# Attention outputs of the samples with two head pairs per matmul, and ten weight splits moved from GpSimd to VectorE

## The chip, the cores and the metric

The kernel runs on one core of a Trainium2 chip. The time is the device time of one execution in microseconds (us). A core has five engines that run side by side, each through its own queue in order: TensorE (PE in the profile; its weight loads are listed apart as PEld), VectorE (DVE), ScalarE (ACT), GpSimd (POOL) and SyncE (SP), which only starts transfers. They wait for each other through semaphores.

## The reference

One inference step of a hybrid encoder layer for one prompt of 512 frames and 8 samples of 16 frames, 640 rows of width 1024:

```python
z = rmsnorm(x) @ w_in                     # columns: u 512, gate 512, q 512, k 128, v 128
lru_out  = rg_lru(causal_conv(u)) * gelu(gate)
attn_out = sliding_window_attention(rmsnorm(q), rmsnorm(k), v, sinks)   # 8 heads of 64, 2 key-value heads
h = x + concat(rmsnorm(lru_out), rmsnorm(attn_out)) @ w_out
y = h + peer(rmsnorm(h))                  # 8 heads, top 16 of 16384 single-neuron experts
```

The attention of a sample reads its 128 cached keys and values and its own 16:

```python
s = einsum('btgrd,bkgd->bgrtk', q, k) * 64 ** -0.5       # 2 groups g, 4 heads r in each
p = sink_softmax(s, sink)
o = einsum('bgrtk,bkgd->btgrd', p, v)                     # 64 x 16 for each sample and head
```

Everything is fp32.

## The kernel before, in words

All matmuls of weights run in three passes over a split: a number is cut into a high part `wh` (type fp32r, made by ScalarE in line 95) and a low rest `wl = raw - wh` (line 100, on the engine that the caller names), and TensorE adds high by high, high by low and low by high. The weights of the projections come as slabs of 128 x 2048. `next_slab(engine)` takes the next slab that SyncE has loaded, issues the high copy on ScalarE and the subtraction on the engine named, and asks SyncE for a further slab. Raw slabs, high parts and low parts have two buffers each.

The order on each engine is the order of the program text; no planner moves anything in the part that is changed. The stages are:

1. 0 to 36 us: keys and values of all rows, projected as the input arrives.
2. 36 to 200 us: the queries of the first four heads, the four slices of `u` with the convolution on VectorE (lines 365 to 376), the gates of the recurrence, its scan, and the prompt's attention in eight pieces (`Prompt`: scores, softmax, division, transposes, outputs), laid between the projections.
3. 200 to 275 us: `merge`, the product with `w_out`, one bank of 512 columns in 12 matmuls of 512 columns (line 622). VectorE takes each bank out into `rows` (line 628) or `h_rows` (line 636). The samples' attention is laid between: class `Samples` for samples 0 to 3 (`sm[0]`) and 4 to 7 (`sm[1]`).
4. 275 to 430 us: queries of the experts and their top keys. 5. 430 us to the end: the dense pass over all experts for the prompt and the gathered rows of the samples.

TensorE writes its results to PSUM. Four banks, tag `pb`, go round among scores, transposes, outputs and merges; two double banks, tag `pa`, serve the projections. A bank comes free when its reader (ScalarE or VectorE) is through.

In `Samples.outputs` the probabilities lie transposed in `pT` (keys by head and frame, 128 columns for a sample), so one key-value group of one sample has 64 neighbouring columns: two halves `hp` of 32, each with two heads of 16 frames. For each sample, group and half, one matmul takes 128 cached values (weights 128 x 64) and a second one the sample's own 16 (weights 16 x 64); both add into the same 64 PSUM partitions, the lower ones for one half and the upper ones for the other, because `oT` wants the heads so. That is 4 x 2 x 2 x 2 = 32 matmuls of 32 columns for one call, and in the trace each fp32 matmul is two passes. ScalarE then copies the whole bank into `oT` (line 580) in one instruction.

Of the kernel before, what the change touches and what calls it, by code (L numbers as in the profile page):

```python
# [12 lines left out]
AF = mybir.ActivationFunctionType  # L13
# [6 lines left out]
S = 512  # L20
NB, TS = 8, 16
# [27 lines left out]
def hybrid_layer(ctx: ExitStack, tc: tile.TileContext, i, o):  # L49
    nc = tc.nc  # L50
    V, A, G, PE = nc.vector, nc.scalar, nc.gpsimd, nc.tensor
# [17 lines left out]
    def bank():  # L69
        return pss.tile([P, 512], F32, name="pb", tag="pb", bufs=4)  # L70
# [22 lines left out]
    def high(raw):  # L93
        wh = stream.tile([P, 2048], F32R, name="wh", tag="wh")
        A.activation(wh, raw, AF.Copy)  # L95
        return wh

    def low(raw, wh, eng):
        wl = stream.tile([P, 2048], F32R, name="wl", tag="wl")
        eng.tensor_sub(wl, raw, wh.bitcast(F32))  # L100
        return wl
# [109 lines left out]
    def fetch_slab():  # L211
        n = len(slab_raw)
        if n < len(order):
            slab_raw.append(load_slab(order[n]))

    def next_slab(eng):

        raw = slab_raw[len(slabs)]
        wh = high(raw)
        slabs.append((wh, low(raw, wh, eng)))  # L220
        fetch_slab()
# [20 lines left out]
    qT, oT = qo[:, 0:4, :], qo[:, 4:8, :]  # L242
# [25 lines left out]
    def project_heads(c, t, s):  # L268
        ps = bank()[:, :256]
        for k in range(KD):  # L270
            project_rows(kc(slabs[s]), k, t, ps)
        heads_rows(c, t, ps)
# [24 lines left out]
    V.tensor_scalar(gqs, small["gq"], HD ** -0.5, None, op0=ALU.mult)  # L297

    project_heads(0, 0, 0)
    next_slab(G)  # L300
    project_heads(0, 1, 0)
    rb1 = rs1.spread(dg1)
    for t in range(2, NT):
# [4 lines left out]
    vown = wk.tile([TS, NB, P], F32, name="vown", tag="twice")  # L308
# [52 lines left out]
    def convolve(ct, ps, amid):  # L361
        u = wk.tile([P, UL], F32, name="u", tag="u", bufs=2)
        G.memset(u[:, 0:3], 0.0)
        G.tensor_copy(segs(u)[:, :, 0:3], small["st_conv"][:, ct])
        V.tensor_mul(u[:, 3:3 + H2], ps[:, 0, :H2], rb1[:, :H2])
        V.tensor_mul(u[:, 3 + H2:S + 3], ps[:, 1, :S - H2], rb1[:, H2:S])
        V.tensor_mul(segs(u)[:, :, 3:], ps[:, 1, S - H2:H2].rearrange("p (b s) -> p b s", s=TS),
                     rb1[:, S:].rearrange("p (b s) -> p b s", s=TS))
        G.tensor_copy(cst[:, ct, 0, :], u[:, S:S + 3])
        G.tensor_copy(cst[:, ct, 1:, :], segs(u)[:, :, TS:])  # L370
        cw = small["conv_w"]
        xc = xcs[ct] = wk.tile([P, UL], F32, name="xc", tag=("xc", "sq")[ct // 2], bufs=2)
        V.tensor_scalar(xc[:, X], u[:, X], cw[:, ct, 0:1], small["conv_b"][:, ct:ct + 1],
                        op0=ALU.mult, op1=ALU.add)
        for j in range(1, 4):
            V.scalar_tensor_tensor(xc[:, X], u[:, j:j + XL], cw[:, ct, j:j + 1], xc[:, X],
                                   op0=ALU.mult, op1=ALU.add)
            if j == 1:
                amid()
# [26 lines left out]
    def lru_weight(pair):  # L406
        for ct in pair:
            r, ig, a, q = rg[ct]
            V.tensor_mul(q[:, X], a[:, X], a[:, X])
            V.scalar_tensor_tensor(q[:, X], q[:, X], 1.0, r[:, X], op0=ALU.add, op1=ALU.mult)  # L410

    def lru_root(pair):
        for ct in pair:
            A.activation(rg[ct][3][:, X], rg[ct][3][:, X], AF.Sqrt)

    def lru_scan(pair):
        for ct in pair:
            r, ig, a, q = rg[ct]
            V.tensor_mul(ig[:, X], ig[:, X], q[:, X])
            G.memset(heads_of(a), 0.0)  # L420
            G.tensor_copy(heads_of(ig), small["st_lru"][:, ct])
            if ct == 0:
                hs["all"] = wk.tile([P, CT, UL], F32, name="hall", tag="hall")
            h = hs[ct] = hs["all"][:, ct]
            V.tensor_tensor_scan(h[:, X], a[:, X], ig[:, X], 0.0, ALU.mult, ALU.add)
            G.tensor_copy(lst[:, ct, 0:1], h[:, S - 1:S])
            G.tensor_copy(lst[:, ct, 1:], segs(h)[:, :, TS - 1])

    def project(s, n, between=()):
        ps = wide()  # L430
        for k in range(KD):
            proj_T(ps, kc(slabs[s]), xh, xl, n, (k,))
            if k < len(between):
                between[k]()
        return ps
# [17 lines left out]
    rows2 = (slice(0, 64), slice(64, 128))  # L453

    class Prompt:
# [49 lines left out]
        def outputs(self):  # L505
            n, nk, k0, hh, pT = self.n, self.nk, self.k0, self.hh, self.pT
            po = bank()[:, :2 * P].rearrange("p (b q) -> p b q", b=2)
            for h4 in range(4):
                for kt in range(nk):
                    PE.matmul(po[rows2[h4 % 2], h4 // 2], v_sb[:, k0 + kt, hh * HD:(hh + 1) * HD],  # L510
                              pT[:, h4, kt, :], start=(kt == 0), stop=(kt == nk - 1))
            A.activation(oT[:, 2 * hh:2 * hh + 2, n * P:(n + 1) * P], po, AF.Copy)
# [5 lines left out]
    class Samples:  # L518
# [43 lines left out]

        def outputs(self):
            pT = self.pT
            po = bank()[:, :4 * 4 * TS]
            pov = po.rearrange("p (a b t) -> p a b t", a=4, b=4)
            for b4 in range(4):
                b = 4 * self.hb + b4
                for g in range(2):
                    gd = slice(g * HD, (g + 1) * HD)  # L570
                    for hp in range(2):
                        c = slice((2 * g + hp) * 32, (2 * g + hp + 1) * 32)
                        out = pov[rows2[hp], 2 * g:2 * g + 2, b4, :]
                        PE.matmul(out, vc[:, b, gd], pT[:, 0, b4, c].rearrange("p (a t) -> p a t", a=2),
                                  start=True, stop=False)
                        PE.matmul(out, vown[:, b, gd], pT[:TS, 1, b4, c].rearrange("p (a t) -> p a t", a=2),
                                  start=False, stop=True)

            c0 = S + self.hb * 4 * TS
            A.activation(oT[:, :, c0:c0 + 4 * TS], po.rearrange("p (a q) -> p a q", a=4), AF.Copy)  # L580


    rows_x, rv_a, rv_h = {}, *[wk.tile([P, NT], F32, name=n) for n in ("rv_a", "rv_h")]
# [42 lines left out]
    def merge_lru_out(hf, t, ps):  # L626
        x = rows_x[t][:, hf * 512:(hf + 1) * 512]
        V.scalar_tensor_tensor(x, ps, rl[:, t:t + 1], x, op0=ALU.mult, op1=ALU.add)

    def merge_lru(hf, t):  # L630
        merge_lru_out(hf, t, merge(L0 + hf, t, 0))

    def merge_attn(hf, t):
        ps = merge(A0 + hf, t, CT)
        cs = slice(hf * 512, (hf + 1) * 512)
        V.scalar_tensor_tensor(h_rows[:, t, cs], ps, ra[:, t:t + 1], rows_x[t][:, cs], op0=ALU.mult, op1=ALU.add)
# [17 lines left out]
    pr[0][0].scores()  # L654
    pr[0][0].softmax()
    convolve(0, pu0, pr[0][0].divide)
    next_slab(G)
    pu1 = project(U0, 1)

    exchange(pr[0][0], pr[0][1])  # L660
    convolve(1, pu1, pr[0][1].divide)
    pu2 = project(U1, 0)
    next_slab(G)

    exchange(pr[0][1], pr[0][2])
    convolve(2, pu2, pr[0][2].divide)
# [5 lines left out]
    for t in range(NT):  # L672
        project_heads(1, t, Q1)
        if t == 1:
            pr[0][3].turn()
            next_slab(G)
            lru_weight(A01)
        if t == 2:
            pr[0][3].outputs()
        if t == 3:  # L680
            lru_root(A01)
    heads_norm(1)
    lru_scan(A01)
    next_slab(G)
    pg = project(G0, 0)
    for u in range(2):
        heads_turn(qkv[1], qT[:, 2 + u], gqs, u)
# [4 lines left out]
    a, b, c, d = pr[1]  # L692
# [9 lines left out]
    sq0 = attn_square(0)  # L702
    lru_decay(A23)
    lru_weight(A23)
    next_slab(G)
    pg = project(G1, 0)
    attn_sum(0, sq0)

# [9 lines left out]
    vc = wk.tile([P, NB, P], F32, name="vc", tag="vc")  # L718
# [33 lines left out]
    sm[0].scores()  # L752
    rs.add(sqs[0])
    rl = rs.rows()
    next_slab(G)
    merge_lru_out(0, 0, ps0)
    ps1 = merge(L0, 1, 0)
    d.turn()
# [11 lines left out]
    sm[1].divide()  # L770
    sm[0].outputs()
    merge_lru_out(0, 3, ps3)
    next_slab(G)
    merge_lru(0, 4)
    sm[1].turn()
    ps0 = merge(L0 + 1, 0, 0)
# [13 lines left out]
    nc.sync.dma_start(o["ncv"], cst)  # L790
    nc.sync.dma_start(o["nlr"], lst)
    merge_lru(1, 4)
    next_slab(G)


    h_rows = big.tile([P, NT, D], F32, name="h_rows", tag="acc")
# [23 lines left out]

    for t in range(NT):
        merge_attn(0, t)
    next_slab(G)
    for t in range(ND):
        merge_attn(1, t)
        nc.sync.dma_start(Hd[t], h_rows[:, t])
# [48 lines left out]
    for name in ("sk1", "sk2"):  # L875
        t = ta.tile([P, NK], F32, name=name)
# [43 lines left out]
    for u in range(2, 2 * PH):  # L920
        c, n = u // 2, u % 2
# [256 lines left out]
    used, c = 0.0, 2  # L1178
# [117 lines left out]
    po = [vps.tile([P, 512], F32, name="po", tag=f"po{k}") for k in range(KD)]  # L1296
# [126 lines left out]
```

## Time and profile before

| what | number |
|---|---|
| three timed runs | 1806.92, 1795.57, 1801.92 us; median 1801.92 |
| the profiled execution | 1800.01 us, its span 1798.2 us |
| DVE busy | 1417.0 us (79%) |
| ACT busy | 689.5 us (38%) |
| POOL busy | 723.0 us (40%) |

An engine's busy share is a mean over stages with different bounds. What a part is worth is read from its own stage: where TensorE, which does most of the work, stands still or runs at its lower clock, and what it waits for there. In the timeline a row may merge several instructions of one line ("x2" behind them); the bracket at its end says how long the engine stood idle in front of it and what released it. The column PEclk of the windows is the granted TensorE clock as a share of 2.4 GHz, so 0.50 is 1.2 GHz.

### The profile page before, as it was taken

The page shows a single profiled execution, that of the slowest core. Times are in us where ns is not written, and L with a number is a line of the kernel's source. Part 1 is how long each engine was busy: PE and PEld are TensorE (multiplying, and loading weights), DVE is VectorE, ACT ScalarE, POOL GpSimd, SP SyncE. Part 2 cuts the span into 40 slices and gives each one's busy share as a digit, 9 for nine tenths or more (in the row PEclk, how much of TensorE's full clock was granted, in tenths as well). Part 3 has the DMA queues.
Part 4 walks back from the last instruction along what each step waited for, and adds up shares of the span by engine and source line. Part 5 has one row for each costly group of instructions (what it writes and reads, how often), then busy time and mean ns, then how long its engine had stood idle before and what let it go on. Part 6 is the DMA issues. An engine that isn't in the chain of part 4 may idle for free.

```text
span 1798.2 us, 24867 instructions
## 1 busy us (share of the span) xinstructions
PE 1710.4 (95%) x9698; PEld 1563.8 (87%) x9698; DVE 1417.0 (79%) x2332; ACT 689.5 (38%) x792; POOL 723.0 (40%) x493
## 2 busy tenths in 40 slices
PE   8989999999999998899999999899999899999998
PEld 7877789998988897888888888899899799999998
DVE  7875435998666988889888877688888788888887
ACT  5456323323444443454455544222322222223232
POOL 5343222321010434344334434465555455554552
PEclk9998889999999999999999999999999999999999
DMA  5212124113454897999799999999999899999995
GB/s 163 97 46 103 41 77 145 61 58 125 169 204 171 311 356 269 309 363 359 253 347 358 356 331 374 412 366 377 373 392 382 332 386 383 379 378 388 383 364 219
DMA packets 180982, 492.68 MB, mean 274 GB/s; under 512 B 16816, under 2 KB 75056, under 8 KB 170224
## 3 DMA queue, kind: packets, MB, share of 16 engines
q1 hardware_dynamic: 58416, 231.01, 35.4%
q0 software_dynamic: 55296, 201.35, 29.2%
q10 hardware_dynamic: 67152, 58.73, 9.6%
q8 instruction: 76, 1.25, 0.3%
q14 instruction: 42, 0.34, 0.1%
HBM read 426.11 MB, written 65.48 MB: 273 GB/s over the span
## 4 chain that ended last, share of the span: by engine, by line
PE 39%; DVE 31%; ACT 8%; issue 8%; DMA 7%; ACTq 2%; POOL 1%; DVEq 0%; SPq 0%; POOLq 0%
PE pa L941 18%; DVE wl L100 9%; DVE h_rows L1162 8%; PE po L1317 6%; PE pa L113 6%; DMA Gd<-stage 4%; PE pb L622 3%; DVE at L1230 3%; ACT ph L1235 3%; DVE h_rows L1157 2%; ACTq L1247 2%; ACT wh L95 2%; DMA at<-Ad 2%; PE pb L1112 2%; DVE ring L1157 2%
## 5 line engine op out<-in xcount | busy, mean ns | idle before, releaser
L941 PE MATMUL pa<-xh,wh 128*128 128x448 f32 x1024 | 382.6, 374 | 27.0 <-ACT act L1244 27.0
L100 DVE TENSOR_TENSOR wl<-raw,wh 128x2048 fp32r<-128x2048 f32 x127 | 290.4, 2288 | 138.4 <-ACT wh L95 137.3
L1317 PE MATMUL po<-ph,wh 128*128 128x448 f32 x1024 | 376.4, 368 | 7.2 <-ACT ph L1235 6.0
L1317 PE MATMUL po<-pl,wh 128*128 128x448 f32 x1024 | 377.7, 369 | 5.8 <-DVE pl L1237 5.8
L941 PE MATMUL pa<-xh,wl 128*128 128x448 f32 x1024 | 377.6, 369 | 4.3 <-DVE wl L100 4.3
L941 PE MATMUL pa<-xl,wh 128*128 128x448 f32 x1024 | 377.7, 369 | 0.0
L1317 PE MATMUL po<-ph,wl 128*128 128x448 f32 x1024 | 376.0, 367 | 0.0
L95 ACT ACTIVATE wh<-raw 128x2048 fp32r<-128x2048 f32 x146 | 280.0, 1918 | 224.5 <-PE po L1317 110.1
L1150 POOL DMA_INDIRECT h_rows<-in_u_rows,rowi x96 | 142.5, 1484 | 340.0 <-DVE h_rows L1157 246.8
L941 PEld LDWEIGHTS pa<-xh,wh 128*128 128x128 f32 x1024 | 194.7, 190 | 46.3 <-ACT act L1244 30.8
L1317 PEld LDWEIGHTS po<-pl,wh 128*128 128x128 f32 x1024 | 193.5, 189 | 26.8 <-DVE pl L1237 10.7
L1317 PEld LDWEIGHTS po<-ph,wh 128*128 128x128 f32 x1024 | 193.6, 189 | 23.7 <-ACT ph L1235 6.4
L941 PEld LDWEIGHTS pa<-xh,wl 128*128 128x128 f32 x1024 | 194.6, 190 | 21.1 <-DVE wl L100 4.7
L1150 POOL DMA_INDIRECT ring<-in_u_rows,rowi x96 | 140.0, 1459 | 172.3 <-DVE ring L1157 149.3
L941 PEld LDWEIGHTS pa<-xl,wh 128*128 128x128 f32 x1024 | 194.9, 190 | 15.6
L1317 PEld LDWEIGHTS po<-ph,wl 128*128 128x128 f32 x1024 | 193.5, 189 | 15.4
L1150 POOL DMA_INDIRECT h_rows<-in_v,rowi x96 | 147.6, 1537 | 144.1 <-DVE h_rows L1162 121.1
L1150 POOL DMA_INDIRECT ring<-in_v,rowi x96 | 148.5, 1547 | 121.6 <-DVE h_rows L1162 100.3
L1235 ACT ACTIVATE ph<-at 128x896 fp32r<-128x896 f32 x64 | 61.0, 953 | 335.9 <-DVE at L1230 335.9
L1244 ACT ACTIVATE act<-pa 128x448 f32<-128x448 f32 x128 | 69.9, 551 | 203.7 <-PE pa L941 197.7
L100 POOL TENSOR_TENSOR wl<-raw,wh 128x2048 fp32r<-128x2048 f32 x19 | 88.2, 4642 | 147.3 <-ACT wh L95 147.3
L1120 ACT ACTIVATE stage<-pb 128x512 f32<-128x512 f32 x112 | 112.0, 1118 | 69.2 <-PE pb L1112 56.8
(270 smaller groups left out, 2563.7 us busy)
## 6 DMA issues: line engine op xcount, KB each, us to landing
raw<-in_u SPq DMA_DIRECT2D x64, 1024.0 KB, 5.8
raw<-in_v SPq DMA_DIRECT2D x64, 1024.0 KB, 8.6
Ad<-act ACTq DMA_DIRECT2D x64, 448.0 KB, 7.0
Gd<-stage ACTq DMA_DIRECT2D x28, 1024.0 KB, 12.3
gt<-Gd SPq DMA_DIRECT2D x64, 448.0 KB, 9.2
at<-Ad SPq DMA_DIRECT2D x64, 448.0 KB, 10.2
raw<-in_w_query SPq DMA_DIRECT2D x8, 1024.0 KB, 4.8
raw<-in_w_out SPq DMA_DIRECT2D x4, 1024.0 KB, 4.7
```

The source lines that it names most:

```text
L95: A.activation(wh, raw, AF.Copy)
L100: eng.tensor_sub(wl, raw, wh.bitcast(F32))
L113: PE.matmul(ps[:, hf, :H2], a[:, k, cs], b[:, k, hf * H2:(hf + 1) * H2], start=(k == 0 and n == 0), stop=(k == KD - 1 and n == 2))
L622: PE.matmul(ps, a[:, k0 + k, ts_], b[:, k, :], start=(k == 0 and n == 0), stop=(k == CT - 1 and n == 2))
L941: PE.matmul(u_ps[c, n][:, :SD], a[:, k, n * P:(n + 1) * P], b[:, k, :SD], start=(k == 0 and m == 0), stop=(k == KD - 1 and m == 2))
L1120: A.activation(d["stage"][:, :, t0:t0 + 4].rearrange("p j t -> p t j"), d[n, f], AF.Copy, scale=1.0 / GSC)
L1150: G.indirect_dma_start(out=rows[n], out_offset=None, in_=table, in_offset=bass.IndirectOffsetOnAxis(ap=rowi[:, c:c + 1], axis=0))
L1157: V.scalar_tensor_tensor(row, row, 1.0, xrow[:, n // NS_], op0=ALU.mult, op1=ALU.mult, accum_out=dots[:, n:n + 1])
L1162: V.scalar_tensor_tensor(y, row, slots[:, c:c + 1], y, op0=ALU.mult, op1=ALU.add)
L1235: A.activation(ph, a2, AF.Copy)
L1244: A.activation(act[c][:, n], u_ps[c, n][:, :SD], AF.Gelu_apprx_tanh)
L1317: PE.matmul(po[k][:, :SD], a[:, j, k * P:(k + 1) * P], b[:, j, :], start=(c == 0 and j == 0 and n == 0), stop=(c == NS - 1 and j == 1 and ...
```

## The change

Ten calls `next_slab(G)` become `next_slab(V)`: the low parts of those ten slabs are now subtracted by VectorE, at the same place of the program text. Nine subtractions stay on GpSimd (slab 11 on, in stage 4).

In `Samples.outputs` one matmul now takes all 64 columns of a group, both halves `hp`, so there are 4 x 2 x 2 = 16 matmuls of 64 columns for one call. The 64 PSUM partitions are now chosen by the parity `up` of the sample. So that every head still ends in its place in `oT`, four VectorE copies, one for each pair of half and parity, move the results (64 partitions by 128 elements each), in place of the one ScalarE instruction.

```diff
     project_heads(0, 0, 0)
-    next_slab(G)
+    next_slab(V)
     project_heads(0, 1, 0)
...
         def outputs(self):
             pT = self.pT
-            po = bank()[:, :4 * 4 * TS]
-            pov = po.rearrange("p (a b t) -> p a b t", a=4, b=4)
-            for b4 in range(4):
-                b = 4 * self.hb + b4
+
+            po = bank()[:, :8 * 2 * TS]
+            pov = po.rearrange("p (h g a b t) -> p h g a b t", h=2, g=2, a=2, b=2)
+            for b2 in range(2):
                 for g in range(2):
                     gd = slice(g * HD, (g + 1) * HD)
-                    for hp in range(2):
-                        c = slice((2 * g + hp) * 32, (2 * g + hp + 1) * 32)
-                        out = pov[rows2[hp], 2 * g:2 * g + 2, b4, :]
-                        PE.matmul(out, vc[:, b, gd], pT[:, 0, b4, c].rearrange("p (a t) -> p a t", a=2),
+                    cols = slice(2 * g * 32, 2 * (g + 1) * 32)
+                    for up in range(2):
+                        b4 = 2 * b2 + up
+                        b = 4 * self.hb + b4
+                        out = pov[rows2[up], :, g, :, b2, :]
+                        PE.matmul(out, vc[:, b, gd], pT[:, 0, b4, cols].rearrange("p (h a t) -> p h a t", h=2, a=2),
                                   start=True, stop=False)
-                        PE.matmul(out, vown[:, b, gd], pT[:TS, 1, b4, c].rearrange("p (a t) -> p a t", a=2),
+                        PE.matmul(out, vown[:, b, gd],
+                                  pT[:TS, 1, b4, cols].rearrange("p (h a t) -> p h a t", h=2, a=2),
                                   start=False, stop=True)
 
-            c0 = S + self.hb * 4 * TS
-            A.activation(oT[:, :, c0:c0 + 4 * TS], po.rearrange("p (a q) -> p a q", a=4), AF.Copy)
+            own = oT[:, :, S + self.hb * 4 * TS:S + (self.hb + 1) * 4 * TS].rearrange(
+                "p a (b u t) -> p a b u t", b=2, u=2)
+            pos_ = po.rearrange("p (h a b t) -> p h a b t", h=2, a=4, b=2)
+            for hp in range(2):
+                for up in range(2):
+                    V.tensor_copy(own[rows2[hp], :, :, up, :], pos_[rows2[up], hp])
...
     convolve(0, pu0, pr[0][0].divide)
-    next_slab(G)
+    next_slab(V)
     pu1 = project(U0, 1)
...
         if t == 1:
             pr[0][3].turn()
-            next_slab(G)
+            next_slab(V)
             lru_weight(A01)
...
```

The other seven places are the same edit: behind the second convolution slice, behind the first scan, behind `lru_weight(A23)`, behind `rs.rows()`, behind the fourth merge, behind `merge_lru(1, 4)` and behind `merge_attn(0, 4)`.

VectorE's queue behind the convolution of slice 0 of `u` (`xc`), in front of the second prompt piece's softmax (`mx`); the piece of the difference:

```order
 L493 TENSOR_TENSOR p<-p,den 128x4x128
 L376 SCALAR_TENSOR_TENSOR xc<-u,conv_w,xc 128x664 x2
+L100 TENSOR_TENSOR wl<-raw,wh 128x2048
 L477 TENSOR_REDUCE mx<-pb 128x2 x2
 L479 SCALAR_TENSOR_TENSOR mx<-mx,nsink 128x4
```

The subtraction now stands between the last two convolution steps and the softmax's maxima; before, it was GpSimd's and VectorE went on at once.

VectorE's queue around the samples' outputs and the merges, before (`psm` are the samples' probabilities, `rows` the merged rows, `xl` the low part of the attention's output):

```order
L553 TENSOR_TENSOR psm<-psm,dens 128x576
L628 SCALAR_TENSOR_TENSOR rows<-pb,rr,rows 128x512 x4
L596 SCALAR_TENSOR_TENSOR xl<-qo,ga,xh 128x512 x4
L601 TENSOR_SCALAR rv_a<-pb 128x1
L628 SCALAR_TENSOR_TENSOR rows<-pb,rr,rows 128x512
L596 SCALAR_TENSOR_TENSOR xl<-qo,ga,xh 128x128 x4
```

And of the change (line 635 was 628, 603 was 596, 608 was 601; `qo` holds `oT`):

```order
L553 TENSOR_TENSOR psm<-psm,dens 128x576
L587 COPY qo<-pb 64x4x2x16 x4
L635 SCALAR_TENSOR_TENSOR rows<-pb,rr,rows 128x512
L100 TENSOR_TENSOR wl<-raw,wh 128x2048
L635 SCALAR_TENSOR_TENSOR rows<-pb,rr,rows 128x512
L587 COPY qo<-pb 64x4x2x16 x4
L635 SCALAR_TENSOR_TENSOR rows<-pb,rr,rows 128x512 x2
L603 SCALAR_TENSOR_TENSOR xl<-qo,ga,xh 128x512 x4
```

The four evictions of merged rows, which stood in a block, now stand behind the copies of the samples' outputs and behind one subtraction.

## Rows read from the trace of the kernel before

**Rows 1.** The page, part 1: busy time, share, instructions of the engines
```profile
PE 1710.4 (95%) x9698; PEld 1563.8 (87%) x9698; DVE 1417.0 (79%) x2332; ACT 689.5 (38%) x792; POOL 723.0 (40%) x493
```

**Rows 2.** Windows: us, busy PE, PEld, DVE, ACT, POOL, then PEclk, DMA share, GB/s
```profile
200.00:220.00 20.00, 20.00 (x115) 16.45 (x114) 2.58 (x6) 4.97 (x13) 0.54 (x1) 0.74 0.08 27
132.00:136.00 4.00, 2.35 (x7) 1.91 (x8) 1.18 (x4) 3.96 (x13) 0.00 (x0) 0.55 0.72 262
```

**Rows 3.** Timeline of PE, where it had stood idle: start, us, line, [idle before <-releaser]
```profile
54.39 1.28 PE L279 MATMUL pb<-ident,qraw 128*128 128x128 f32 x10 [2.13 <-DVE sp L333]
83.59 0.82 PE L393 MATMUL pb<-xc,wi 128*128 128x332 f32 x2 [1.09 <-ACT p L485]
121.07 1.28 PE L279 MATMUL pb<-ident,qraw 128*128 128x128 f32 x10 [1.16 <-DVE qraw L265]
133.65 1.47 PE L393 MATMUL pb<-xc,wi 128*128 128x332 f32 x2 [5.45 <-ACT p L485]
171.26 0.38 PE L468 MATMUL pb<-mask_k,mask_q 64*128 64x256 f32 x1 [2.21 <-DVE rv_a L601]
```

**Rows 4.** The page, part 5: the subtraction of the low parts on each engine
```profile
L100 DVE TENSOR_TENSOR wl<-raw,wh 128x2048 fp32r<-128x2048 f32 x127 | 290.4, 2288 | 138.4 <-ACT wh L95 137.3
L100 POOL TENSOR_TENSOR wl<-raw,wh 128x2048 fp32r<-128x2048 f32 x19 | 88.2, 4642 | 147.3 <-ACT wh L95 147.3
```

**Rows 5.** Timeline of DVE, 40 to 160 us: instructions beside GpSimd's subtractions, and alone
```profile
40.42 3.26 DVE L295 TENSOR_TENSOR kn<-qraw,gkb 128x256 f32<-128x256 f32 x1
...
59.80 0.28 DVE L367 TENSOR_TENSOR u<-pa,rb 128x128 f32<-128x128 f32 x1
...
62.68 6.17 DVE L376 SCALAR_TENSOR_TENSOR xc<-u,conv_w,xc 128x664 f32<-128x664 f32 x2
...
86.17 1.85 DVE L376 SCALAR_TENSOR_TENSOR xc<-u,conv_w,xc 128x664 f32<-128x664 f32 x2
...
106.04 5.13 DVE L410 SCALAR_TENSOR_TENSOR q<-q,rg 128x664 f32<-128x664 f32 x1
...
126.87 4.20 DVE L479 SCALAR_TENSOR_TENSOR mx<-mx,nsink 128x4 f32<-128x4 f32 x1
...
157.31 1.29 DVE L477 TENSOR_REDUCE mx<-pb 128x2 f32<-128x512 f32 x2 [1.34 <-PE pb L469]
158.64 2.40 DVE L479 SCALAR_TENSOR_TENSOR mx<-mx,nsink 128x4 f32<-128x4 f32 x1
```

**Rows 6.** Chain of work that ended last, 133 to 140 us: start, us, line
```profile
133.65 1.47 PE pb L393 x2
135.12 1.60 PE pa L113 x6
...
139.41 0.56 PE pb L393 x2
139.97 0.88 PE pa L113 x6
```

**Rows 7.** Timeline of PE: starts of both output calls, and prompt outputs of 128 columns
```profile
77.41 1.14 PE L510 MATMUL pb<-pT,v_sb 128*64 128x128 f32 x16
...
203.74 0.30 PE L574 MATMUL pb<-pTs,vc 128*64 128x32 f32 x2
...
203.97 0.30 PE L576 MATMUL pb<-pTs,vown 16*64 16x32 f32 x2
...
221.73 0.30 PE L574 MATMUL pb<-pTs,vc 128*64 128x32 f32 x2
```

**Rows 8.** Chain of work that ended last: the merges behind the outputs, and later ones
```profile
213.01 5.17 PE pb L622 x12
...
231.48 4.53 PE pb L622 x12
...
236.79 35.52 PE pb L622 x156
```

**Rows 9.** Timeline of ScalarE: the high copy behind the fourth merge
```profile
218.22 1.92 ACT L95 ACTIVATE wh<-raw 128x2048 fp32r<-128x2048 f32 x1 [4.79 <-PE pb L622]
```

More of the change, by code (lines that the diff above doesn't have):

```diff
@@ L675, in hybrid_layer @@
             pr[0][3].turn()
-            next_slab(G)
+            next_slab(V)
             lru_weight(A01)
@@ L683, in hybrid_layer @@
     lru_scan(A01)
-    next_slab(G)
+    next_slab(V)
     pg = project(G0, 0)
@@ L704, in hybrid_layer @@
     lru_weight(A23)
-    next_slab(G)
+    next_slab(V)
     pg = project(G1, 0)
@@ L754, in hybrid_layer @@
     rl = rs.rows()
-    next_slab(G)
+    next_slab(V)
     merge_lru_out(0, 0, ps0)
@@ L772, in hybrid_layer @@
     merge_lru_out(0, 3, ps3)
-    next_slab(G)
+    next_slab(V)
     merge_lru(0, 4)
@@ L792, in hybrid_layer @@
     merge_lru(1, 4)
-    next_slab(G)
+    next_slab(V)
     h_rows = big.tile([P, NT, D], F32, name="h_rows", tag="acc")
@@ L822, in hybrid_layer @@
         merge_attn(0, t)
-    next_slab(G)
+    next_slab(V)
     for t in range(ND):
```

## The prediction

> **What bounds the kernel now.** I read the page first, then windows of 20 us, then the waits of TensorE and VectorE in the windows that stood out. TensorE is busy 95% of the span [rows 1], so a change pays only where TensorE stands still, where it does work that goes away, or where it runs at its lower clock. All that is edited lies between 36 and 275 us; from there on the program is the same, and whatever TensorE gains by then moves everything behind it forward.
>
> Two things are to be seen there. First, TensorE stands idle at five points [rows 3], and at four of them what released it hangs on VectorE's queue. VectorE in turn loses time whenever GpSimd subtracts: an instruction of four elements per row takes 4.20 us beside such a subtraction, two steps of the convolution 6.17 us where the same two take 1.85 us alone [rows 5]. The excess, 4.0 and 4.3 us, is nearly GpSimd's whole 4.64 us [rows 4]: VectorE does not run slower, it is held until GpSimd is through. Secondly, between 200 and 240 us TensorE is never idle, yet its clock is 0.74 of full over 200 to 220 us [rows 2]; this is where the samples' outputs run.
>
> **The sum, part 1: the subtractions.** VectorE needs 2.29 us for what GpSimd does in 4.64 us [rows 4]. Where the two collided, VectorE therefore trades a hold of 4 us or more for 2.29 us of its own. Along the chain:
>
> - Slab 1. VectorE's `kn` took 3.26 us beside GpSimd. It has 256 elements per row; 128 take 0.28 us [rows 5], so some 0.5 us alone. Then 3.26 - 0.5 - 2.29 = 0.5 us are won, and the stall at 54.39 us shrinks by 0.5.
> - Slabs 2 and 3. Each pair of convolution steps loses 6.17 - 1.85 = 4.3 us of hold and gets 2.29 us of subtraction: 2.0 us each, so VectorE and the softmax behind it are over 3 us earlier near 82 us. The stall of 1.09 us at 83.59 us [rows 3], a wait for a bank that ScalarE's exponentials read, goes wholly. TensorE is 1.6 us ahead.
> - Slab 4. `q` (line 410) took 5.13 us; at 128 x 664 it takes like a convolution step 0.92 us alone [rows 5]. 5.13 - 0.92 - 2.29 = 1.9 us; some 0.6 us of it is lost because VectorE now waits in its queue for ScalarE's high copy, which GpSimd used to wait for. 1.3 us stay, VectorE is 2.9 us ahead. The square roots and the queries of the last row tile then are late next and pass on 2.5 us, so the stall of 1.16 us at 121.07 us shrinks to 0.2 and TensorE is 2.5 us ahead.
> - Slab 5. The maximum's rescaling took 4.20 us where a free one takes about 0.2 us: 4.2 - 0.2 - 2.29 = 1.7 us. The stall of 5.45 us shrinks to 3.7 us, and TensorE is 2.5 + 1.7 = **4.2 us** ahead.
> - Slab 6. The rescaling took 2.40 us. The reductions (1.29 us and a small one, 1.5 us together) that ran beside GpSimd's subtraction now run behind VectorE's: 4.64 - 2.29 - 1.5 = **0.8 us**, off the stall of 2.21 us at 171.26 us.
> - Slab 7 to 10 stand among the merges, where TensorE has no such stalls. I cost them at nothing. Cover: a merge lasts 35.52 / 13 = 2.73 us [rows 8] and four banks go round, so an eviction may come two merges late before TensorE waits.
>
> Behind the stall of 5.45 us TensorE ran at 0.55 of full clock [rows 2]. From 133.65 to 139.41 us it did two rounds of two gate and six projection matmuls, 5.76 us; a round at full clock is 0.56 + 0.88 = 1.44 us [rows 6]. The fall cost 5.76 - 2.88 = 2.9 us. Whether 3.7 us of idleness still make it fall no row tells. So nothing or 2.9 us comes back; I take half, **1.4 us**.
>
> **Part 2: the outputs.** One call lasts from 203.74 to 213.01 us, 9.27 us, the other from 221.73 to 231.48 us, 9.75 us [rows 7, 8]; together 19.0 us. At full clock a matmul of two passes with 32 columns starts 203.97 - 203.74 = 0.23 us behind the one before. Sixteen of these remain per call. If columns cost nothing, a call takes 16 x 0.23 = 3.7 us; if the time goes with the columns, 7.3 us. I take the first end with a little added: the prompt's outputs, 128 columns with weights of the same form, need only 1.14 / 16 = 0.07 us per pass [rows 7] against 0.115 here, so the time is not in the columns, and six passes of 320 columns in 0.88 us [rows 6] give 0.46 ns per column, hence 32 x 2 x 0.46 = 0.03 us per matmul. 16 x 0.26 = 4.1 us per call; 19.0 - 8.2 = **10.8 us** won, bounds 19.0 - 14.6 = 4.4 and 19.0 - 7.4 = 11.6.
>
> The Trainium skill, "TensorEngine Tiling (Array Packing)", section Instruction Overhead, says that a matmul has some 60 cycles of overhead, so that one column is as dear as sixty. By that the call would take an estimated 16 x 0.23 x 64/60 = 3.9 us and the sum would be 0.4 us more; the trace's 0.07 us for 128 columns is nearer to that than to proportional cost.
>
> The merges behind both calls ran at the low clock, 5.17 and 4.53 us where one takes 2.73: 2.4 + 1.8 = 4.2 us. The first fall came in the middle of the call; a call half as long may end before the clock falls or at that moment. Again between nothing and 4.2 us, half: **2.1 us**.
>
> **Part 3: the copies.** Four copies of 128 elements cost about 0.28 us each [rows 5], 1.1 us per call, and ScalarE is rid of one instruction. Behind them on VectorE stand the eviction of merge (0,3), then the subtraction of slab 8, which must wait for ScalarE's 1.92 us copy behind the fourth merge [rows 9], then the eviction of merge (0,4): it comes 1.92 + 2.29 = 4.2 us later than now. Waiting for that bank would be the third merge on; between lie eight transposes, a merge of 2.73 us and 4.1 us of outputs. Hidden; without the cover it would cost 4.2 us once. The readers of `oT` get it 0.7 us later and TensorE needs their result two merges on.
>
> **Sum**: 4.2 + 0.8 + 1.4 + 10.8 + 2.1 = 19.3 us, 1800.0 - 19.3 = **1780.7**, say 1781 us. The profiled execution, 1800.01 us, lies 1.9 us under the median of the runs, 1801.92 us, well inside their spread of 11 us.
>
> **The rivals.**
>
> A. *The forecast*, 1777 to 1786 us: chance 0.52.
>
> B. *The low clock stays and columns cost.* Part 1 gives 5.0 us, no clock comes back, the calls take nearer 7.3 us: 5.0 + 4.4 = 9.4, 1790.6 us. For it: short matmuls are still what runs there, and the clock fell in both calls. Against: the 128-column row. Chance 0.22.
>
> C. *VectorE's queue eats part 1*: the subtractions wait for ScalarE in front of urgent work, as slab 4's does. Only part 2 remains, 12.9 us, 1787 us. Against: the holds of 4 us are on the page as times, and they go for certain. Chance 0.15.
>
> D. *GpSimd is held instead.* The hold works both ways if the one that starts first wins: then VectorE's 2.29 us delay GpSimd's small instructions on the chain, the powers of `heads_norm` in front of the stalls at 54.39 and 121.07 us. At most 2 x 2.29 = 4.6 us go back, 1785.3 us. The Trainium skill, "SBUF — State Buffer", section Who interferes with whom, has this rule: a VectorE instruction with two inputs in SBUF and a GpSimd instruction that reads SBUF lock each other out, whichever comes second. The trace agrees on VectorE's side (4.20 us for four elements); no row shows GpSimd held for long. Against: in the new order both powers start behind the subtraction's end. Chance 0.06.
>
> E. *Slower: VectorE becomes the bound from 36 to 275 us.* If the held instructions were waiting for something else anyway, nothing comes back for the ten subtractions, 22.9 us; four of them wait for ScalarE's 1.92 us first, 7.7 us, and the copies add 8 x 0.28 = 2.2 us. 32.8 - 10.8 = 22 us more, 1822 us. It decides once VectorE's evictions lag two merges, 5.5 us, behind TensorE. Against: VectorE is busy 2.58 of 20 us where the merges begin [rows 2]. Chance 0.05.
>
> **The numbers.** The likeliest is A, **1781 us**. B and C lie under the top of the range; with 5 us of spread on either side of A's full gain (all clock back: 22.8 us, 1777 us) and of B I get **1771 to 1796 us**. Within 1% is what a measurement of this kernel cannot tell from no change: 18 us, above 1784 us. A lies mostly past that, D and C mostly not: faster by over 1% 0.52, within 1% 0.43, slower 0.05.
>
> **What would show it.** Right: no VectorE instruction of a few elements over 1 us between 40 and 160 us; the stall at 83 us gone, the one at 121 us under 0.5 us, the one at 133 us near 3.7 us; each call of the outputs about 4 us for 32 passes; merges behind them at 2.7 us. Wrong: passes of the new matmuls at twice 0.115 us, a granted clock of 0.5 behind the calls as before, TensorE waiting on VectorE's `rows` between 190 and 260 us, or VectorE idle for ScalarE's high copy in front of the softmax.

## The result, and the profile after

The changed kernel takes **1776.13 us** (median of 4 runs, 1773.37 to 1778.53), the kernel before on the same chip 1800.36 us (4 runs, 1795.57 to 1806.92): ratio **0.9862**, 95% interval 0.9826 to 0.9899. Measured a second time, in other runs of both kernels, it was 0.987 (0.9833 to 0.9906). The profiled execution took 1778.0 us with a span of 1776.2 us, 22.0 us less than before. Of the kernels below, two of the six runs of the one with three changes took 3247 and 5580 us, for which I have no cause; they count in its median and not in its ratio.

The page's first part answers [rows 1]. TensorE loses 9.7 us of busy time, and its share of the shorter span is 96% in place of 95%; GpSimd loses 35.3 us, VectorE 2.5 us, though it took over ten subtractions of 2.29 us: more time went out of its other rows than subtraction came in.

```profile
PE 1700.7 (96%) x9634; PEld 1553.2 (87%) x9634; DVE 1414.5 (80%) x2350; ACT 688.8 (39%) x790; POOL 687.7 (39%) x483
```

TensorE's timeline, where it had stood idle (start, us, line, idle before and what ended it). Of the five stalls of [rows 3] three are left, of 0.80, 3.62 and 0.80 us; those of 1.09 and 1.16 us are gone:

```profile
52.36 1.28 PE L279 MATMUL pb<-ident,qraw 128*128 128x128 f32 x10 [0.80 <-DVE sp L333]
127.31 1.47 PE L393 MATMUL pb<-xc,wi 128*128 128x332 f32 x2 [3.62 <-ACT p L485]
164.22 0.38 PE L468 MATMUL pb<-mask_k,mask_q 64*128 64x256 f32 x1 [0.80 <-DVE rv_a L608]
```

VectorE's timeline, the instructions of [rows 5] that had stood beside GpSimd's subtractions: 3.26 has become 0.41 us, 6.17 has become 1.85, 5.13 has become 0.85, 4.20 has become 0.17, 2.40 has become 0.16.

```profile
39.65 0.41 DVE L295 TENSOR_TENSOR kn<-qraw,gkb 128x256 f32<-128x256 f32 x1
...
60.64 1.85 DVE L376 SCALAR_TENSOR_TENSOR xc<-u,conv_w,xc 128x664 f32<-128x664 f32 x2
...
105.49 0.85 DVE L410 SCALAR_TENSOR_TENSOR q<-q,rg 128x664 f32<-128x664 f32 x1
...
121.59 2.27 DVE L100 TENSOR_TENSOR wl<-raw,wh 128x2048 fp32r<-128x2048 f32 x1
...
124.56 0.17 DVE L479 SCALAR_TENSOR_TENSOR mx<-mx,nsink 128x4 f32<-128x4 f32 x1
...
153.82 0.16 DVE L479 SCALAR_TENSOR_TENSOR mx<-mx,nsink 128x4 f32<-128x4 f32 x1
```

The chain of waits through the outputs (start, us, line), against [rows 7, 8]. A call now runs from 197.46 to 201.56 us, 4.10 us for 16 matmuls of two passes; the other, from 209.72 to 213.82 us, also 4.10 us. The merge behind the first call is still slow, 4.54 us, the one behind the second is not, 2.95 us. The long row of merges starts at 217.56 in place of 236.79 us: **19.2 us** earlier.

```profile
197.46 0.26 PE pb L576 x2
197.72 0.25 PE pb L578 x2
...
201.56 4.54 PE pb L629 x12
...
209.72 0.26 PE pb L576 x2
...
213.82 2.95 PE pb L629 x12
...
217.56 35.52 PE pb L629 x156
```

The windows (us, busy PE, PEld, DVE, ACT, POOL, then PEclk, DMA share, GB/s) against [rows 2]: the granted clock over 200 to 220 us rose from 0.74 to 0.91 (it is 0.72 over 201 to 207 us, where the slow merge runs, and 1.00 over the second call and its merge); behind the stall of 3.62 us it fell as it had behind 5.45 us.

```profile
200.00:220.00 20.00, 20.00 (x108) 15.79 (x108) 9.95 (x17) 7.13 (x12) 0.00 (x0) 0.91 0.26 83
...
128.00:132.00 4.00, 4.00 (x13) 3.31 (x12) 0.80 (x2) 2.87 (x5) 0.00 (x0) 0.50 0.02 4
```

### The profile page after: what moved, and what is told of

Same layout as the page of the kernel before. It is cut to its first block, busy times and chain, and to the rows that moved or that the text cites. A ratio compares the mean times of both kernels' runs of the same rounds, so it can differ in the third digit from the quotient of the medians.

```text
span 1776.2 us, 24745 instructions
## 1 busy us (share of the span) xinstructions
PE 1700.7 (96%) x9634; PEld 1553.2 (87%) x9634; DVE 1414.5 (80%) x2350; ACT 688.8 (39%) x790; POOL 687.7 (39%) x483
## 4 chain that ended last, share of the span: by engine, by line
PE 54%; DVE 20%; DMA 7%; ACT 7%; issue 5%; ACTq 2%; POOL 1%; DVEq 0%; SPq 0%; POOLq 0%
PE po L1324 24%; PE pa L948 16%; PE pa L113 6%; DMA Gd<-stage 5%; DVE wl L100 5%; PE pb L629 3%; DVE h_rows L1169 3%; DVE h_rows L1164 2%; DVE ring L1164 2%; ACTq L1254 2%; ACT stage L1127 2%; ACT wh L95 2%; DMA gt<-Gd 2%; PE pb L1119 1%; DVE at L1237 1%
## 5 line engine op out<-in xcount | busy, mean ns | idle before, releaser
L100 DVE TENSOR_TENSOR wl<-raw,wh 128x2048 fp32r<-128x2048 f32 x137 | 313.2, 2287 | 141.6 <-ACT wh L95 135.8
L1157 POOL DMA_INDIRECT ring<-in_u_rows,rowi x96 | 145.3, 1514 | 160.9 <-DVE ring L1164 137.8
L1244 DVE TENSOR_TENSOR pl<-at,ph 128x896 fp32r<-128x896 f32 x64 | 69.9, 1092 | 72.9 <-ACT ph L1242 72.9
```

What stands on the lines that cost most here:

```text
L1157: G.indirect_dma_start(out=rows[n], out_offset=None, in_=table, in_offset=bass.IndirectOffsetOnAxis(ap=rowi[:, c:c + 1], axis=0))
L1244: V.tensor_sub(pl, a2, ph.bitcast(F32))
```

## The experiments

Whole times of one kernel differ by up to 20 us from run to run (before, on one chip: 1789.11 to 1809.14 us), so each kernel is also read at a mark in its trace, behind which nothing is edited. It is the matmul of the dense pass (line 941 before, 948 after) that waits some 4.3 us for a low part of VectorE; the expectations call it the first block of the dense pass. That line's first matmul runs 25.5 us earlier (at 407.43 us before, 388.19 us after), and distances read there are the same within 0.03 us, but for the kernel with all subtractions on VectorE. A second mark, VectorE's line 265, lies ahead of every edit and starts between 35.99 and 37.97 us; "net" is the distance between the two, less that of before (432.94 - 37.60 = 395.34 us).

| Kernel | Median, us (before on the same chip) | Ratio, 95% interval | Dense pass, us | Net, us | From there to the end |
|---|---|---|---|---|---|
| before | 1800.36 | | 432.94 | 0 | 1365.3 |
| the change | 1776.13 (1800.36) | 0.986, 0.983 to 0.990 | 413.68 | -18.5 | 1362.5 |
| the change again | 1775.23 (1799.45) | 0.987, 0.983 to 0.991 | 413.31 | -19.6 | 1361.4 |
| outputs only | 1784.89 (1795.12) | 0.994, 0.992 to 0.996 | 418.23 | -13.1 | 1365.8 |
| subtractions only | 1787.74 (1795.12) | 0.995, 0.994 to 0.997 | 426.43 | -6.9 | 1366.8 |
| added subtractions | 1789.35 (1799.45) | 0.995, 0.992 to 0.998 | 423.45 | -8.1 | 1359.0 |
| added memsets | 1775.14 (1799.45) | 0.987, 0.981 to 0.993 | 413.59 | -18.5 | 1353.5 |
| late low parts | 1773.72 (1795.12) | 0.987, 0.984 to 0.990 | 407.61 | -24.0 | 1366.4 |
| sorted | 1773.03 (1795.12) | 0.988, 0.985 to 0.992 | 407.64 | -25.0 | 1359.7 |
| pairs apart, sorted | 1775.25 (1799.65) | 0.988, 0.984 to 0.992 | 411.69 | -21.3 | 1359.3 |
| all on VectorE | 1801.49 (1799.65) | 1.001, 0.998 to 1.004 | 437.55 | +5.0 | 1364.4 |
| late, sorted, added | 1769.57 (1799.45) | 0.984, 0.980 to 0.988 | 403.15 | -28.4 | 1366.7 |
| late, sorted, three changes | 1776.01 (1799.65) | 0.985, 0.980 to 0.991 | 403.01 | -28.7 | 1363.6 |
| late, sorted, one change | 1766.50 (1796.40) | 0.982, 0.979 to 0.985 | 401.74 | -30.0 | 1355.7 |

The last column, the same program everywhere, goes from 1353.5 to 1366.8 us in no order: the 2.8 us that the first profile won there are not shown to be the change's.

**The change again.** The changed kernel, unedited.

> The changed kernel once more, as the measure for the others here. Up to the first block of the dense pass (413.68 us in its first profile, 19.3 us earlier than before the change) it should repeat within 1 us. If the 2.8 us that its first profile won behind that point belong to the change, they are there again and the ratio is 0.986; if they come and go with the run, as behind the other three kernels (+0.5, +1.5, +1.1 us), the span from there on is within 3 us of the one before the change.

The mark came at 413.31 us. Its line 265 starts at 37.60 us as in the profile before, so the two can be laid on each other; the section on the prediction does that.

**Outputs only**, the ten calls back to `next_slab(G)`.

> The merged outputs and VectorE's copies stay, all ten subtractions go back to GpSimd. If the two parts of the change add up independently: the five stalls of TensorE stand as before the change (2.1, 1.1, 1.2, 5.5, 2.2 us), the two calls last 4.1 us each in place of 9.3 and 9.8, and the merge behind the second runs at full clock; 10.9 + 2.2 = 13 us less than before, about 1787 us. Rival, the calls are short only because TensorE comes to them otherwise: one or both calls stay above 6 us and the time is above 1791 us. Rival, the gain of the whole change is all here: 1776 us.

The first theory. The stalls are 2.06, 1.09, 1.17, 5.45 and 2.21 us; the first call lasts 4.28 us (its last two matmuls are slow), the second 4.10 us, the merges behind them 4.27 and 2.97 us.

**Subtractions only**, `outputs()` and ScalarE's copy as before.

> The ten subtractions are VectorE's, the samples' outputs and ScalarE's copy are those of before the change. If the parts add up: the stalls are 1.3, none, none, 3.6 and 0.8 us, the calls of the outputs start 6.4 us earlier than before and last 9.3 and 9.8 us; 1800.4 - 6.4 = 1794 us. Rival, the 2.8 us that the changed kernel wins behind 420 us come from the subtractions too: 1791 us. Rival, what is won in front of 200 us is lost again among the merges, where VectorE now subtracts between evictions: 1800 us.

The calls start at 197.20 us, 6.5 us earlier than before, last 9.14 and 9.64 us, and the gain is kept: net -6.9. The parts add: 13.1 + 6.9 = 20.0 beside 18.5 and 19.6 us.

**Added subtractions: is it a hold?** GpSimd subtracts beside slabs 2 to 6 once more, into a spare tile whose content nobody reads.

```diff
         slabs.append((wh, low(raw, wh, eng)))
+        if 3 <= len(slabs) <= 7:
+            G.tensor_sub(spare, raw[:, :m], wh.bitcast(F32)[:, :m])
```

> The changed kernel, with a subtraction on GpSimd added beside each of the slabs 2 to 6, of the same inputs, into a spare tile that nobody reads (2048 elements per row for slabs 2 to 4, some 4.6 us; 1280 for slabs 5 and 6, some 2.9 us). Theory, VectorE is held while GpSimd subtracts: the two convolution steps beside it last 6 us again in place of 1.85, the rescaling of the maximum behind slab 5 over 2 us in place of 0.17, the stall at 127.31 us grows from 3.6 to 6 us or more and the first block of the dense pass comes at 417 to 421 us in place of 413.7; 1780 to 1784 us. Rival, what was won is only that the subtraction itself is finished sooner: nothing waits for the added ones, no instruction of VectorE is longer, 1776 us.

**Added memsets.** In place of the subtraction `G.memset(spare, 0.0)`, twice or three times.

> As the kernel with the added subtractions, but GpSimd fills the spare tile with zeros instead, two or three times, some 3.8 us per slab: as long, and without reading. Theory, it is GpSimd's reading beside VectorE's instructions of two inputs that holds VectorE: no instruction of VectorE is longer than in the changed kernel, 1776 us. Rival, any long instruction of GpSimd holds it, or its writing does: the steps last 5 to 6 us, 1780 to 1784 us.

VectorE's and GpSimd's timelines of the kernel with the added subtractions:

```profile
59.99 4.59 POOL L225 TENSOR_TENSOR hall<-raw,wh 128x2048 f32<-128x2048 f32 x1 [2.25 <-ACT wh L95]
60.07 6.17 DVE L382 SCALAR_TENSOR_TENSOR xc<-u,conv_w,xc 128x664 f32<-128x664 f32 x2
...
107.69 2.29 DVE L100 TENSOR_TENSOR wl<-raw,wh 128x2048 fp32r<-128x2048 f32 x1 [0.58 <-ACT wh L95]
107.78 6.67 POOL L225 TENSOR_TENSOR hall<-raw,wh 128x2048 f32<-128x2048 f32 x1 [5.71 <-issue]
109.89 5.26 DVE L415 TENSOR_TENSOR q<-rg 128x664 f32<-128x664 f32 x1
```

The same two engines in the kernel with the memsets:

```profile
68.92 3.91 POOL L226 MEMSET hall<- 128x2048 f32 x2
71.12 0.91 DVE L383 SCALAR_TENSOR_TENSOR xc<-u,conv_w,xc 128x664 f32<-128x664 f32 x1
...
125.42 3.61 POOL L226 MEMSET hall<- 128x1280 f32 x3
126.00 0.16 DVE L484 SCALAR_TENSOR_TENSOR mx<-mx,nsink 128x4 f32<-128x4 f32 x1
```

Two convolution steps take 6.17 us again beside a subtraction whose result nobody reads; beside memsets nearly as long (3.91 and 3.61 us) a step takes 0.91 and the rescaling 0.16 us, as alone. So it is a hold, and it comes from GpSimd's subtracting. At 107.78 us it is to be seen in both directions: GpSimd starts 0.09 us behind VectorE's subtraction and takes 6.67 in place of 4.6 us, then VectorE's next instruction takes 5.26 in place of 0.84. Behind this chain of holds TensorE waits 4.19 us for `qraw`, which I had not expected; at 68.49 us, behind the first added subtraction, it had waited 2.76 us for a low part. The mark comes at 423.45 us, past my 417 to 421, and the median of 1789.35 us is past my 1784. The rescaling behind slab 5 takes 2.38 us, as expected, but the stall there did not grow to 6 us: TensorE comes to it later and waits 3.33 us.

TensorE's timeline of the kernel with the added subtractions:

```profile
68.49 0.67 PE L113 MATMUL pa<-xh,wl 128*128 128x320 f32 x2 [2.76 <-DVE wl L100]
...
125.95 1.54 PE L284 MATMUL pb<-ident,qraw 128*128 128x128 f32 x10 [4.19 <-DVE qraw L270]
...
138.92 0.83 PE L399 MATMUL pb<-xc,wi 128*128 128x332 f32 x2 [3.33 <-ACT p L489]
```

The Trainium skill, "SBUF — State Buffer", section Who interferes with whom, has the rule that a VectorE instruction with two inputs in SBUF and a GpSimd instruction that reads SBUF exclude each other, and that one which only writes does not take part; these rows agree: VectorE is held, GpSimd is held, and beside the memset nothing is.

**Late low parts.** What is left of the largest stall is VectorE's own subtraction in front of the softmax's reduction.

```diff
     lru_scan(A01)
-    next_slab(V)
+    wh5 = next_high()
...
     a.divide()
+    next_low(wh5, V)
     pg = project(G0, 1, lru_gates(A23))
```

and the same for slab 6, from in front of `project(G1, 0)` to behind `c.divide()`. `next_high` issues ScalarE's copy at the old place, `next_low` the subtraction at the new one.

> The changed kernel, with the subtractions of slabs 5 and 6 on VectorE put behind the next softmax's division instead of in front of its reduction. Theory, VectorE's own 2.28 us of subtraction is what is left of the stall at 127.31 us: the stall shrinks from 3.62 to 1.4 us and the one of 0.80 us goes. If TensorE's clock falls behind 1.4 us of idleness as well, 1776 - 2.2 - 0.8 = 1773 us; if it does not, 2.8 us more, 1770 us. Rival, ScalarE's table load and exponentials are what is late there: the stall stays at 3.0 us or more and the time at 1776 us.

TensorE's timeline of that kernel, and its window behind the stall:

```profile
124.77 0.82 PE L403 MATMUL pb<-xc,wi 128*128 128x332 f32 x2 [1.63 <-ACT p L495]
...
158.89 1.15 PE L520 MATMUL pb<-pT,v_sb 128*64 128x128 f32 x16 [0.80 <-DVE rv_a L618]
```

```profile
128.00:132.00 4.00, 4.00 (x24) 3.53 (x23) 0.49 (x1) 1.90 (x4) 1.36 (x1) 1.00 0.64 199
```

The stall is 1.63 us and the granted clock stays at 1.00: all four kernels with this edit show both (1.63 or 1.64 us). In the nine kernels that stand idle 3.6 or 5.45 us there, the clock behind it is below 0.75 over 4 us. The tenth, that with the added subtractions, falls to 0.50 behind an idleness of 4.19 us and stays at 1.00 behind one of 3.33 us 13 us later. The stall of 0.80 us did not go, it moved to 158.89 us (`rv_a`), so that term of mine was wrong; and the next wait, for `xh` from ScalarE, grew from 1.59 to 2.88 us, which gives part of the gain back. Net it wins 4.4 to 5.5 us on the change; the ratio of the whole times, 0.987, does not show it through what the runs differ by.

**Sorted.** First all products with the cached values, then all with the own ones:

```diff
-            for b2 in range(2):
-                for g in range(2):
...
+            for own_keys in range(2):
+                for up in range(2):
+                    for b2 in range(2):
...
+                        for g in range(2):
...
+                            PE.matmul(out, (vown if own_keys else vc)[:, b, gd],
+                                      pT[:n, own_keys, b4, cols].rearrange("p (h a t) -> p h a t", h=2, a=2),
...
```

In this kernel the own products are not added to all of the cached ones, so its sums are incomplete and it serves for the time alone; the instructions are the same in number and shape.

> The changed kernel, with the 16 matmuls of a call in another order: first the eight with the cached values (128 rows of weights), then the eight with the own ones (16 rows), the four of one half of the bank behind each other. Theory, the 0.13 us of a pass is the price of changing between two forms of weights from one matmul to the next: 32 passes come to 0.07 us as in the prompt's outputs, a call to 2.3 to 2.6 us, the time to 1776 - 3 = 1773 us. Rival, it is the price of a short pass whatever stands beside it: 4.1 us per call, 1776 us.

**Pairs apart, sorted.** The pairs of heads as before the change, 32 columns, but sorted.

> The changed kernel with the pairs of heads apart again, as before the change (32 columns per matmul, 32 matmuls of two passes per call), but sorted: first the sixteen with the cached values, then the sixteen with the own ones, these in the other half of the bank and added by VectorE. Theory, what a pass of the old order cost (0.115 us) is mostly the change of the weights' form: the 64 passes come to 0.05 to 0.06 us each, a call to 3.2 to 3.6 us, less than the 4.1 us of the merged pairs in the old order, and the first block of the dense pass to 412 to 414 us. Rival, a short pass costs 0.115 us by itself, and only their number counts: 7.4 us per call, 420 us.

The chains of waits of the two, the first and its call and merge:

```profile
197.60 1.79 PE pb L578 x32
199.39 2.96 PE pb L629 x12
```

```profile
196.56 3.55 PE pb L575 x64
200.10 4.53 PE pb L625 x12
...
208.25 3.54 PE pb L575 x64
211.79 2.97 PE pb L625 x12
```

1.79 / 32 = 0.056 us per pass with 64 columns, 3.55 / 64 = 0.055 us with 32: **in this order columns cost nothing at this size**. In the old order, at full clock as well, a pass took 0.115 us with 32 columns and 4.10 / 32 = 0.128 us with 64. What is over goes with the changes from weights of 128 rows to weights of 16 and back: (4.10 - 1.79) / 14 = 0.165 us for each change less. It is not the adding to the place that was written last: in the change's chain a matmul that adds there (0.26 us behind the one before) and one that goes to another place (0.25 us) cost the same.

Before the change a call at full clock would have taken 32 x 0.23 = 7.36 us; the merged pairs won 3.26 us of it, 3.55 - 1.79 = 1.76 us for thirty-two passes less and 1.5 us for sixteen changes less. The other 1.9 and 2.4 us of the two calls were the clock, which fell in the middle of the long calls. Sorting alone, with the pairs apart, gives 3.55 us, less than the change's 4.10. The Trainium skill, "TensorEngine Tiling (Array Packing)", section Key Properties, says that changing the tiling mode drains the engine; these rows agree that a change costs time, though they name no mode and show no drain.

**All on VectorE**, the nine remaining subtractions too.

> The changed kernel with the remaining nine subtractions (those of the queries' projections and the first two of the dense pass, 275 to 430 us) on VectorE as well. Theory, the hold is what counts: nine times VectorE trades a hold for 2.29 us of its own; but there VectorE, with the searches of the maxima, is busy over 90% and ends last in front of the dense pass, and only the instructions of two SBUF inputs are held, of which there are few: VectorE takes up to 9 x 2.29 = 20 us more, and the first block of the dense pass comes at 420 to 433 us in place of 413.5. Rival, the searches are held too, by over 2.3 us per subtraction: 413 us or less.

The mark came at 437.55 us, 24 us later than in the change: more than the 9 x 2.29 = 20 us of subtraction, and past my range. The first matmul of the dense pass comes 19.8 us later, at 407.94 us; the rest is a longer wait at the dense pass's low parts, 7.8 in place of 4.3 us. TensorE now also waits for `wl` among the queries' projections, where it had not waited (what waits, for what: us, times, longest):

```profile
PE pa L113 <- DVE wl L100: 11.7, 6, 2.0
PE pa L948 <- DVE wl L100: 7.8, 2, 6.8
```

The searches were never held: the other kinds, too, take 276 to 285 ns in both kernels. Grouped by shape over 275 to 435 us (busy us, mean ns of one, idle before), this row stands both in the change, where GpSimd subtracts eight times beside them, and here, where it doesn't:

```profile
L911 DVE MAX8 val<-s 128x8 f32<-128x128 f32 x80 | 23.6, 295 | 2.8
```

**Late and sorted together**, in three forms. In the first the own products go to the other half of the bank and VectorE adds them:

> The changed kernel with both further edits: the subtractions of slabs 5 and 6 behind the next softmax's division, and the matmuls of a call sorted by form of weights, the products with the own values in the other half of the bank and added by VectorE when it copies. Theory, the two gains add up: 6.1 us at the first block of the dense pass from the one, 6.0 us from the other, which then starts near 401.6 us, 31 us earlier than before the change; 1776 - 12 = 1764 us. Rival, with the eight additions on VectorE and the late subtractions its queue delays the evictions of the merges: TensorE waits there for VectorE and 3 us or more go back, 1767 us or more.

In the second they accumulate in place, `start` on the first matmul of each half alone, and the halves of the bank are done one after the other:

> The changed kernel with both further edits and without the additions: in each half of the bank the four matmuls with the cached values and then the four with the own ones, accumulated in place, only the first of them starting the sum. Three changes of form per call in place of fifteen. From 4.10 us with fifteen and 1.79 us with one, a change costs 2.31 / 14 = 0.165 us: a call lasts 2.1 us. The first block of the dense pass comes at 401 to 402 us (403.1 with the additions, whose 2.5 us of VectorE stood in front of a merge), the time is 2 us less than with the additions, 1766 us beside 1800. Rival, the price goes with the number of columns or passes and not with the changes: a call of 3 us or more.

In the third the cached products of both halves come first:

> As the kernel with late subtractions and one start per half, but all eight matmuls with the cached values come first, over both halves of the bank, then the eight with the own ones: one change of form per call in place of three. If the call goes with the changes, it is 1.79 us again in place of 2.42 and the first block of the dense pass comes at 401.7 us in place of 403.0; 1765 to 1770 us, beside 1800. Rival, the changes of the half cost as much as those of the form: 2.4 us per call and 403.0 us.

The calls last 1.79, 2.42 and 1.79 us, the mark comes at 403.15, 403.01 and 401.74 us. The first two miss the 401.6 and the 401 to 402 us that I had expected. The additions cost what the second form loses in its calls: in the first, VectorE's eight copies and additions stand on the chain from 202.80 to 205.3 us. In the second a change costs more than my 0.165 us: (2.42 - 1.79) / 2 = 0.3 us. It is not the half of the bank, which changes three times in the third form and once in the second; why one price does not fit all changes is open. The third form meets its 401.7 us; its net gain of 30.0 us is the sum of its parts (18.5 to 19.6 of the change, then 4.4 to 5.5 and 5.4 to 6.5, together 29.4 to 30.5), and **1766.50 us, 0.982 (0.979 to 0.985)**, is the lowest ratio here, though the whole times do not set it apart from the first form's. Its chain through the outputs:

```profile
191.73 1.79 PE pb L588 x32
193.51 2.96 PE pb L640 x12
...
205.63 35.52 PE pb L640 x156
```

## Why the prediction was right, point by point

It forecast a sum of 19.3 us. The second profile of the change, which starts as the one before does, has 19.6 us at the dense pass (net; the first has 18.5). The median of the runs is 24 us down, and its 1776.13 us lies just below the 1777 to 1786 us of A; what is more than the 19.6 lies where runs differ anyway and is not shown to be the change's. That the sum came so near is in part luck: the five stalls gave 6.7 us in place of 5.0, the clock behind the long one about 1 us in place of 1.4 (in the first profile nothing), and 0.7 us were lost for which it had no term. By its steps, before against that second profile:

- **Slab 1**: the stall at 54.39 us went from 2.13 to 0.90 us, 1.2 us and not 0.5. `kn` takes 0.41 us, which gives 0.56; the other 0.7 is what I missed: the 0.51 us that VectorE stood idle among the rows of heads are gone, and this part of its queue is through 1.24 us earlier (line 262 starts at 47.67 in place of 48.91 us).
- **Slabs 2 to 4**: the stalls of 1.09 and 1.16 us are gone; I had left 0.2 of the second. VectorE's wait for the high copy in front of slab 4 is 0.58 us, as forecast (0.6).
- **Slab 5**: 3.62 us left, 3.7 forecast. TensorE restarts at 128.09 in place of 133.65 us, 5.6 us ahead and not 4.2.
- **Slab 6**: the stall of 2.21 us became 0.80, 1.4 us and not 0.8; TensorE leaves it at 163.82 in place of 171.26 us, 7.4 us ahead. The 1.34 us for which VectorE had waited for the scores in front of these maxima [rows 5] are gone too: its subtraction now falls there, which I had not counted.
- **Clock behind the stall of slab 5**: I took half of 2.9 us, between two ends with no row to choose by. The first two rounds of gates and projections last from 128.09 to 132.63 us, 4.54 in place of 5.76 us, but a third is slow as well: about 1 us came back. In the first profile, 127.31 to 133.09 us, nothing did. That step stays a guess: 3.6 us of idleness let the clock fall every time, and what the fall cost differed from run to run.
- **A term I did not have**: between the stall of slab 6 and the first call 0.7 us are lost again (the calls start 6.7 us earlier, at 197.08 in place of 203.81 us on the chain); the granted clock is 0.50 over 172 to 184 us there. The five points of the prediction leave out three idle times of before in this stretch, 1.42, 0.79 and 1.33 us between 175 and 188 us; 1.59, 0.33 and 0.26 us stand there now, so it is not idleness that grew.
- **The calls**: 4.09 and 4.10 us, as forecast; 10.8 us won, as forecast. A matmul takes 0.256 in place of 0.23 us at full clock, which fits the 0.03 us that I had added for the columns. The reason was half right: the time is not in the columns, but of the 0.23 us that I gave to a matmul two sorted passes are 0.11 us, and the other half is the change between the two weights' forms.
- **The merges behind them**: 4.54 and 2.97 us, 2.2 us won; I took half of 4.2. It is the second merge that came back nearly whole; with merged pairs and sorted calls both did (2.96 and 2.97 us), with the pairs apart and sorted the first did not (4.53 us).
- **The copies** cost nothing: 1.20 us per call, and the eviction of merge (0,4), behind slab 8's subtraction at 208.08 us, delays no matmul: TensorE is busy for all of 200 to 220 us.
- **The signs**: one of the wrong ones was there, VectorE idle for ScalarE's high copy in front of a softmax, for 0.50 us at 150.23 us; the stall of that slab shrank all the same. One of the right ones was not met in full: `den`, four elements per row, takes 1.15 us at 95.65 us beside another GpSimd instruction, `rg` (line 402), which the change leaves where it was.

Of the rivals, B fell with the calls (the low clock stayed only behind the first), C and E with the subtractions-only kernel, which kept its gain. D's hold of GpSimd exists, but not where it was feared: the two powers still take 3.5 us each. In the change, a copy of one element per row takes 2.17 us beside VectorE's subtraction at 121.59 us, where the same took 0.73 us alone. No engine waits for it.

```profile
119.07 0.73 POOL L426 COPY lst<-hall 128x1 f32<-128x1 f32 x1 [1.64 <-DVE hall L425]
...
121.74 2.17 POOL L426 COPY lst<-hall 128x1 f32<-128x1 f32 x1 [1.64 <-DVE hall L425]
```

## What to carry to other kernels

Where a short instruction of VectorE with two SBUF inputs lasts as long as GpSimd's subtraction beside it, moving the subtraction to VectorE costs less than leaving it, but only where VectorE has room and its neighbours are of that kind; beside the searches the same move lost 24 us. Put what is moved behind the work that somebody waits for, not in front of it. For short matmuls count the changes between weights of different height before the columns: sorting them gave more than merging them.

## What the runs showed of the hardware

- A VectorE instruction with two SBUF inputs and a GpSimd subtraction hold each other for a whole instruction, whichever comes second: 6.17 in place of 1.85 us on VectorE, 6.67 in place of 4.6 us on GpSimd; memsets of 3.9 us hold nothing.
- A matmul pass with 64-wide weights takes 0.055 us with 32 and 0.056 us with 64 columns at full clock, and a change between 128 and 16 rows of weights 0.165 us as the mean over fourteen, 0.3 us over two; one price for all is not shown.
- The length of an idle time does not tell by itself whether the granted clock falls. In front of the gates behind slab 5 it fell behind 3.6 us in all seven kernels that had it and behind 1.63 us in none of four. But in the kernel with the added subtractions it fell behind 2.76 us (0.50 over 70 to 72 us) and not behind 3.33 us; and behind 0.89 us at 52.25 us it fell in the kernel with the memsets (0.50 over 56 to 58 us), while behind 0.90 us at the same place of the change's second profile it stayed at 1.00.
